# The low part of Q on both partition halves: a second score matmul with 128 rows

## The chip, the cores and the metric

The kernel runs on one core of a Trainium2 chip. The metric is the device time of one execution in microseconds (us). Engines are named as the profile names them: PE is the matmul engine, PEld its weight loads, DVE, ACT and POOL the three elementwise engines, SP the engine whose queue issues every DMA of this kernel.

## The reference, cut to what matters

One encoder layer is computed for a prompt of 512 tokens and a sample of 2048 tokens, both of width 1024. One projection of the normalised input yields everything; branch A is neighbourhood attention on a grid of 64 columns, 8 heads of 64 channels, a window of 8 x 16 keys, a learned bias; branch B is a 2-D DFT, branch C a depthwise convolution. The three are gated, merged and projected.

```python
q, k, v, gate_a, u_b, gate_b, c_val, c_glu, gate_c, merge_a, merge_b, merge_c = split(h @ w_in)
s = einsum('bqhd,bikhd->bhqik', q_row * 64 ** -0.5, k_blk) + bias        # per head, masked to the window
p = softmax(s)
y_a = einsum('bhqik,bikhd->bqhd', p, v_blk) * silu(gate_a)
```

## The kernel before, in words

All matmul operands are held as two float32r parts, high and low, whose sum is the float32 value. A product of two such numbers is high by high, high by low and low by high; the low by low term is left out in most places.

The work is done in chunks of 512 tokens: chunk 0 is the prompt, chunks 1 to 4 the sample. A first pass projects chunks 1 and 2 together, then 3 and 4, then 0; a second pass merges and projects out. Q, K and V leave each projection for DRAM (`qd`, `kd`, `vd`) and come back for attention. `proj_qk` (L282) stores K with one DMA per high and low part (L310), Q with one DMA (L307).

`attention(c)` (L485) is a generator with 112 steps per chunk. It runs over four pairs of heads j; a pair loads its K (`ksp`, L528) and its Q (`qsp`, L530 to L534), both in a single buffer, so that the load for pair j+1 waits for the last score matmul of pair j. Then come four column blocks cb, each with a V load (`vsp`, L545, two buffers) and two heads h. A head's scores come from two matmuls, L553 and L554, over 2, 3 or 4 times 128 keys, so 256, 384 or 512 columns. K of a head holds its high part on partitions 0 to 63 and its low part on 64 to 127. The high part of Q stands on both halves, so L553 gives high Q by high K plus high Q by low K with 128 rows. L554 adds low Q by high K with 64 rows. DVE adds the bias and takes the maximum (L557), ACT exponentiates and scales (L561, L563), PE transposes (L584), and PE multiplies with V (L594) some heads later.

There are 5 chunks with 4 pairs each, so 20 loads of Q, and 20 x 8 = 160 score pairs of L553 and L554.

`task` and `pump` (L255 to L268) mix the steps of generators into the projections: after every six projection matmuls, `pump` emits as many attention steps as are due. The framework's scheduler then orders each engine's queue with a timing model of its own, so the order in the trace isn't quite the source's order. All DMAs stand in one SP queue in that order.

The 20 pairs are numbered 0 to 19 below: 0 to 3 belong to chunk 1, 4 to 7, 8 to 11 and 12 to 15 to chunks 2, 3 and 4, and 16 to 19 to the prompt. The first and second score pair of a head pair are those of cb = 0 with h = 0 and h = 1.

Of the kernel before, what the change touches and what calls it, by code (L numbers as in the profile page):

```python
# [15 lines left out]
F32 = mybir.dt.float32  # L16
# [11 lines left out]
C = 512            # tokens of a chunk: 8 grid rows  # L28
NCH = 5            # chunk 0 is the prompt, 1..4 the sample
# [3 lines left out]
# row patterns of attention: (key quads, first key row relative to the row group - 4, key row of the grid)  # L33
# [7 lines left out]
def attention_masks():  # L41
    """Additive masks [row pattern, query, column pattern, key] of the window."""
    out = np.full((4, P, 3, 512), -1e30, np.float32)
    for mp, (rows, r0, kr0, nq) in enumerate(((8, 0, 0, 2), (32, 0, 0, 3), (32, 8, 4, 4), (32, 24, 20, 3))):
        for cp, cb in enumerate((0, 1, 3)):
            for q in range(P):
                r, c = r0 + q // 16, 16 * cb + q % 16
                rs = min(max(r - 4, 0), rows - 8)
                cs = min(max(c - 8, 0), 48)
                kr = kr0 + np.arange(nq * 4)[:, None]  # L50
                kc = KSTART[cb] + np.arange(32)[None, :]
                ok = (kr >= rs) & (kr < rs + 8) & (kc >= cs) & (kc < cs + 16)
                out[mp, q, cp, : nq * 128] = np.where(ok, 0.0, -1e30).reshape(-1)
    return out.astype(ml_dtypes.bfloat16)


def dft_pairs(n1):
    """The residues k1 of a unit of the position DFT; the others are mirrored ones."""
    h = n1 // 2
    return [(0, h)] + [tuple(range(k, min(k + 2, h))) for k in range(1, h, 2)]  # L60


def dft_tables():
    """Units [128, (k1 of the pair, real and imaginary input, real and imaginary output, 128)], L = 2048 and 512."""
    units = []
    p = np.arange(P, dtype=np.float64)[:, None]
    k2 = np.arange(P, dtype=np.float64)[None, :]
    for n1 in (16, 4):
        L = n1 * P
        for pair in dft_pairs(n1):  # L70
            u = np.zeros((P, 2, 2, 2, P))
            for i, k1 in enumerate(pair):
                a = 2 * np.pi * np.mod(p * (k1 + n1 * k2), L) / L
                c, s = np.cos(a) / math.sqrt(L), np.sin(a) / math.sqrt(L)
                u[:, i, 0, 0], u[:, i, 0, 1] = c, -s
                if k1 % (n1 // 2):
                    u[:, i, 1, 0], u[:, i, 1, 1] = -s, -c
            units.append(u.reshape(P, 1024))
    return np.stack(units).astype(np.float32)
# [12 lines left out]
class Build:  # L92
# [5 lines left out]
    def newton(self, pool, tag, v, eng, steps=3, bufs=2):  # L98
        """v -> 1/sqrt(v) on a tile, through the exponent trick and Newton steps."""
        nc = self.nc  # L100
        shape = list(v.shape)
        y = pool.tile(shape, F32, tag=tag, name="nw_y", bufs=bufs)
        t = pool.tile(shape, F32, tag=tag, name="nw_t", bufs=bufs)
        nc.vector.tensor_scalar(y.bitcast(I32), v.bitcast(I32), 1, None, op0=ALU.logical_shift_right)
        nc.vector.tensor_scalar(y.bitcast(I32), y.bitcast(I32), -1, 0x5F3759DF, op0=ALU.mult, op1=ALU.add)
        if shape[1:] == [1]:
            w = pool.tile(shape, F32, tag=tag, name="nw_w", bufs=bufs)
            nc.vector.tensor_scalar_mul(w, v, -0.5)
            for _ in range(steps):
                nc.vector.tensor_scalar(t, y, y, w, op0=ALU.mult, op1=ALU.mult)  # L110
                nc.vector.scalar_tensor_tensor(y, t, 1.5, y, op0=ALU.add, op1=ALU.mult)  # L111
            return y
        for _ in range(steps):
            eng.tensor_tensor(t, y, y, op=ALU.mult)
            nc.vector.scalar_tensor_tensor(t, t, -0.5, v, op0=ALU.mult, op1=ALU.mult)
            nc.vector.scalar_tensor_tensor(y, t, 1.5, y, op0=ALU.add, op1=ALU.mult)
        return y

    def split(self, dst, src):
        """dst[:, 0] + dst[:, 1] = src."""  # L120
        nc = self.nc
        nc.scalar.copy(dst[:, 0], src)  # L122
        return nc.vector.tensor_tensor(dst[:, 1], src, dst[:, 0].bitcast(F32), op=ALU.subtract)  # L123

    def emit_unit(self, src, pieces=1):
        """A [128, 1024] weight unit, split into its two parts."""
# [8 lines left out]
    def unit(self):  # L135
        """The next unit of the stream; the two behind it are on their way."""
# [4 lines left out]
    def stream(self):  # L141
        """The units of the first pass in their order."""
# [10 lines left out]
    def narrow(self, ps, w, rhs, kts=range(KT)):  # L153
        """ps[128 cols, C] = sum over kts of w[kt]^T rhs[kt], three passes."""
# [11 lines left out]
    def wide(self, ps, ws, lhs, tt):  # L166
        """ps[128 tokens, 256] = sum over kt of lhs[kt][:, tokens]^T w[kt]."""
# [13 lines left out]
    def rstd_rows(self, c, pool, xpool, tag, bufs):  # L181
        """rstd of every token of chunk c, into DRAM as a row; returned by token too."""
# [12 lines left out]
    def make_h(self, c, pool, tiles, ring):  # L195
        """Appends the ring tiles of chunk c: h^T, split."""
# [12 lines left out]
    def raw_h(self, c, tiles, ring):  # L209
        """As make_h, but without rstd: the users of these tiles scale their results."""  # L210
# [18 lines left out]
    def raw_scale(self, c, pool, rrow):  # L229
        """rstd of chunk c, by token (self.rt) and as a row on all partitions (self.rr)."""  # L230
# [24 lines left out]
    def task(self, gen, n, start, end):  # L255
        """Emits gen's n steps evenly between the half units start and end."""
# [17 lines left out]
    def scaled(self, c, ps):  # L274
        """A projection of chunk c from tiles without rstd gets it here."""
# [6 lines left out]
    def proj_qk(self, hs):  # L282
        nc = self.nc
        for j in range(4):
            for dst in (self.kd, self.qd):
                w = self.unit()
                for c, hT in hs.items():
# [12 lines left out]
                    if dst is self.qd:  # L300
                        # the queries of a column block together
# [51 lines left out]
    def proj_c(self, hs, first=()):  # L353
        """first: PSUM tags of the first blocks, where others than mm."""
# [22 lines left out]
    def halo(self, left, right):  # L377
        """Fills the borders of two neighbouring chunks; None stands for the end of the sequence."""
# [43 lines left out]
    def conv(self, c, cb, tail=False):  # L422
        """With tail, the columns that need the right neighbour come in a step of their own, the 21st."""
# [61 lines left out]
    def attention(self, c):  # L485
# [4 lines left out]
        # rows of K by chunk: (chunk, first row in it, rows, first row in the tile)  # L490
# [31 lines left out]
        for j in range(4):  # L522
            kn = 4 * nq * 64
            # K of a head: its high part on one half of the partitions, its low part on the other
# [4 lines left out]
            # Q: the high part of either head on both halves, the low parts of both on the first  # L529
# [4 lines left out]
            nc.sync.dma_start(qsp[:64, 2:].bitcast(F32), lo)  # L534
# [4 lines left out]
            for cb in range(4):  # L539
# [8 lines left out]
                for h in range(2):  # L548
# [5 lines left out]
                    nc.tensor.matmul(s[:, :n], lhsT=qsp[:64, 2 + h, cb], rhs=kk[:64], start=False, stop=True)  # L554
# [35 lines left out]
    def attend(self, c, j, cb, h, nq, vsp, psp, pv, o):  # L590
        """pv[V's high part, V's low part; head; P's high part, P's low part], the latter two added into o."""
# [14 lines left out]
    def fft(self, pool, n1):  # L606
        """The 2-D DFT of the prompt (n1 = 4) or of the sample (n1 = 16)."""
# [12 lines left out]
        for blk in range(2):  # L620
# [4 lines left out]
            # G[k1] as pairs (real part, minus the imaginary part)  # L625
# [12 lines left out]
            else:  # L638
# [9 lines left out]
                # d = b1-b7, b2-b6, b3-b5 ; e = the sums ; f = b'1-b'3, b'1+b'3  # L648
# [68 lines left out]
            def stage_o(i, hs):  # L717
                """The real parts' and the imaginary parts' share: their sum, and their difference mirrored."""
# [32 lines left out]
    def prepare(self, c, hh, pool):  # L751
        """The gated branches of 256 tokens, split."""
# [21 lines left out]
    def merge(self, c, hh, ysp, pool, thp):  # L774
        """The merged branches of 256 tokens, transposed and split (4 times their value)."""
# [25 lines left out]
    def finish(self, c, hh, msp, pool, last):  # L801
        nc = self.nc
        for tt in range(2):
# [16 lines left out]
            # the merged sum carries a factor of 4, the guard 16 with it  # L820
# [14 lines left out]
    def dft_parts(self):  # L835
        """The units of the position DFT, split, into DRAM."""
# [5 lines left out]
    def bias_tables(self):  # L842
        """Bias of (head, query (r, c), key row, key column): Toeplitz in rows and columns."""
# [9 lines left out]
    def run(self):  # L853
        tc, nc, a = self.tc, self.nc, self.a
        with ExitStack() as ctx:
# [31 lines left out]
            # the table of functions is loaded while the first data are on their way  # L887
# [13 lines left out]
            # slots of a half: c 32, q and k 64, v 32, u 16, gates 64, merge gates 192 by two halves  # L901
# [12 lines left out]
            # the first two chunks start before their rstd is known  # L914
# [19 lines left out]
            # first super-chunk  # L934
# [23 lines left out]
            # second  # L958
# [23 lines left out]
            # third: the prompt  # L982
# [62 lines left out]
    def constants(self, cst):  # L1045
# [7 lines left out]
        # the gated input of the convolution carries a factor of 2  # L1053
# [57 lines left out]
```

## Time and profile before

| | |
|---|---|
| Time, median of 3 runs | 2563.64 us (2562.47 to 2572.91) |
| Span of the profiled execution | 2565.2 us |
| Mean granted PE clock | 0.926 of full speed |
| PE busy | 2228.6 us (87%), 11184 matmuls |
| PEld busy | 1836.6 us (72%) |
| DVE busy | 1298.2 us (51%) |
| ACT busy | 779.7 us (30%) |
| POOL busy | 295.9 us (12%) |
| DMA | 399.19 MB, mean 156 GB/s; 47.8% of 16 engines' span |

The profiled execution has no time of its own beside its span; the span lies 1.6 us above the median of the three runs. Matmuls are pipelined, so two neighbours in the trace overlap and the distance between their starts is what one costs. A DMA's time on the SP queue is the time that its issue took, not its transfer. In a table by windows, the DMA share is that of all 16 DMA engines, so 0.13 is two of them.

### The profile page before, as it was taken

Reading aid. Unit: us, or ns where it says so; the run is one execution under the profiler, and the core shown is the slowest. Engines: PE = TensorE matmul, PEld = TensorE weight load, DVE = VectorE, ACT = ScalarE, POOL = GpSimd, SP = SyncE. Lnnn points to the kernel's source line nnn. Section 1 sums busy time; section 2 is a strip of 40 time slices with the busy share of each in tenths; the row PEclk is TensorE's granted clock in tenths of the full one; section 3 lists DMA queues with packets and bytes.
Section 4 is the critical chain, followed back from the end, with each engine's and each line's share of the span. In section 5 each row is a group of like instructions: output and inputs, shape, how many; then the busy total and the mean of one; then the engine's idle time right before and its main releaser. Section 6 shows DMA issues by size and latency. Waiting matters only on the chain. (4 is left out here: it accounts for less than half of the span.)

```text
span 2565.2 us, 30454 instructions
## 1 busy us (share of the span) xinstructions
PE 2228.6 (87%) x11184; PEld 1836.6 (72%) x11184; DVE 1298.2 (51%) x2704; ACT 779.7 (30%) x1479; POOL 295.9 (12%) x286
## 2 busy tenths in 40 slices
PE   8869999999989987887878877766887899999998
PEld 7649877777767875665656655555766788898997
DVE  6235565554344464544443422454764357666665
ACT  5113233333322233433333333322344332111111
POOL 0000010100000011111111101100111012122221
PEclk9889999999999998888888888887998999999999
DMA  7346443443623444343333443436655576555542
GB/s 272 103 148 188 159 160 120 159 150 115 188 75 116 156 148 129 118 142 129 128 119 121 146 148 120 151 119 195 215 176 194 188 265 213 180 177 182 174 156 80
DMA packets 238068, 399.19 MB, mean 156 GB/s; under 512 B 33888, under 2 KB 136928, under 8 KB 235232
## 3 DMA queue, kind: packets, MB, share of 16 engines
q1 hardware_dynamic: 237920, 397.26, 47.8%
q8 instruction: 88, 1.44, 0.2%
q14 instruction: 60, 0.49, 0.1%
HBM read 287.61 MB, written 112.73 MB: 156 GB/s over the span
## 5 line engine op out<-in xcount | busy, mean ns | idle before, releaser
L160 PE MATMUL mm<-hT,w 128*128 128x512 f32 x1760 | 741.1, 421 | 51.2 <-DVE z L295 25.6
L161 PE MATMUL mm<-hT,w 128*128 128x512 f32 x1760 | 722.3, 410 | 0.1
L162 PE MATMUL mm<-hT,w 128*128 128x512 f32 x1760 | 720.1, 409 | 0.8 <-DVE w L123 0.8
L160 PEld LDWEIGHTS mm<-hT,w 128*128 128x128 f32 x1760 | 348.3, 198 | 145.0 <-DVE z L295 26.6
L162 PEld LDWEIGHTS mm<-hT,w 128*128 128x128 f32 x1760 | 348.7, 198 | 83.3 <-issue 2.5
L161 PEld LDWEIGHTS mm<-hT,w 128*128 128x128 f32 x1760 | 349.1, 198 | 69.1 <-issue 1.8
L511 POOL TENSOR_TENSOR bias<-tab,mask 128x384 f32<-128x384 f32 (+2 forms) x160 | 182.7, 1143 | 1623.6 <-DVE m L557 1360.9
L123 DVE TENSOR_TENSOR w<-wraw,w 128x1024 fp32r<-128x1024 f32 (+1 forms) x162 | 203.2, 1255 | 129.8 <-ACT w L122 129.3
L434 DVE SCALAR_TENSOR_TENSOR acc<-cb,cw,acc 128x512 f32<-128x512 f32 (+1 forms) x300 | 242.6, 811 | 2.4
L557 DVE CUSTOM_DVE_ANT_0 p<-s,bias 128x384 f32<-128x384 f32 (+2 forms) x160 | 92.8, 581 | 273.7 <-PE s L554 168.6
L122 ACT CAST w<-wraw 128x1024 fp32r<-128x1024 f32 (+1 forms) x162 | 168.1, 1039 | 141.3 <-PE mm L162 87.6
L160 PE MATMUL mm<-ysp,wb 128*128 128x256 f32 x640 | 181.9, 284 | 4.0 <-DVE th L790 4.0
L161 PE MATMUL mm<-ysp,wb 128*128 128x256 f32 x640 | 181.7, 284 | 0.0
L162 PE MATMUL mm<-ysp,wb 128*128 128x256 f32 x640 | 181.6, 284 | 0.0
L561 ACT ACTIVATE p<-p,m 128x384 f32<-128x384 f32 (+2 forms) x160 | 102.0, 638 | 200.4 <-DVE m L560 197.9
L594 PE MATMUL pv<-psp,vsp 128*128 128x256 f32 x512 | 102.2, 315 | 58.7 <-issue 37.5
L174 PE MATMUL mm<-w,hT 128*128 128x256 f32 x480 | 136.9, 287 | 16.2 <-ACT w L122 14.5
L553 PE MATMUL s<-ksp,qsp 128*128 128x384 f32 (+2 forms) x160 | 63.2, 395 | 93.3 <-DMA qsp<-qd 75.1
L594 PEld LDWEIGHTS pv<-psp,vsp 128*128 128x128 f32 x512 | 86.1, 209 | 75.9 <-issue 52.1
L175 PE MATMUL mm<-w,hT 128*128 128x256 f32 x480 | 137.4, 287 | 0.7 <-DVE w L123 0.7
L176 PE MATMUL mm<-w,hT 128*128 128x256 f32 x480 | 136.8, 285 | 0.0
L160 PEld LDWEIGHTS mm<-ysp,wb 128*128 128x128 f32 x640 | 123.3, 193 | 5.6 <-DVE th L790 4.2
(151 smaller groups left out, 3029.1 us busy)
## 6 DMA issues: line engine op xcount, KB each, us to landing
wraw<-wn SPq DMA_DIRECT2D x135, 512.0 KB
vsp<-vd SPq DMA_DIRECT2D x256, 128.0 KB
th<-z SPq DMA_DIRECT2D x120, 256.0 KB
th<-th SPq DMA_DIRECT2D x80, 384.0 KB
tab<-tabd SPq DMA_DIRECT2D x40, 384.0 KB
qsp<-qd SPq DMA_DIRECT2D x60, 256.0 KB
w<-dftd SPq DMA_DIRECT2D x14, 1024.0 KB
kd<-zs SPq DMA_DIRECT2D x40, 256.0 KB
```

The lines of the kernel that those rows point to most:

```text
L122: nc.scalar.copy(dst[:, 0], src)
L123: return nc.vector.tensor_tensor(dst[:, 1], src, dst[:, 0].bitcast(F32), op=ALU.subtract)
L160: nc.tensor.matmul(ps, lhsT=w[:, 0, s], rhs=r[:, 0], start=n == 0, stop=False)
L161: nc.tensor.matmul(ps, lhsT=w[:, 0, s], rhs=r[:, 1], start=False, stop=False)
L162: nc.tensor.matmul(ps, lhsT=w[:, 1, s], rhs=r[:, 0], start=False, stop=n == len(kts) - 1)
L174: nc.tensor.matmul(ps, lhsT=r[:, 0, q], rhs=w[:, 0, s], start=kt == 0, stop=False)
L175: nc.tensor.matmul(ps, lhsT=r[:, 0, q], rhs=w[:, 1, s], start=False, stop=False)
L176: nc.tensor.matmul(ps, lhsT=r[:, 1, q], rhs=w[:, 0, s], start=False, stop=kt == KT - 1)
L434: nc.vector.scalar_tensor_tensor(acc[:, :n], cb[:, b, e:e + n], wv[:, e:e + 1], acc[:, :n], op0=ALU.mult, op1=ALU.add)
L511: nc.gpsimd.tensor_tensor(bias, tabs[h][:, trow: trow + 4 * nq, RCOL[cb]: RCOL[cb] + 32], mask[:, COLPAT[cb], :n].rearrange("p (r c) -> p ...
L561: nc.scalar.activation(p[:, :n], p[:, :n], AF.Exp, bias=m[:, 1:2], accum_out=m[:, 2:3])
L594: nc.tensor.matmul(pv[:, h], lhsT=vsp[:, i, h], rhs=psp[:, i], start=i == 0, stop=i == nq - 1)
```

## The change

The third load of Q, which put the low parts of both heads on partitions 0 to 63, becomes two loads, one per head, each of which puts a head's low part on both halves. They have the form of the two loads of the high part and alternate with them. L554 takes all 128 rows; it now also adds low Q by low K. The diff also drops comments, which are left out here.

```diff
             for h in range(2):
                 nc.sync.dma_start(qsp[:, h].bitcast(F32), hi[:, h].unsqueeze(0).broadcast_to([2, 64, C]))
-            nc.sync.dma_start(qsp[:64, 2:].bitcast(F32), lo)
+                nc.sync.dma_start(qsp[:, 2 + h].bitcast(F32), lo[:, h].unsqueeze(0).broadcast_to([2, 64, C]))
...
                     nc.tensor.matmul(s[:, :n], lhsT=qsp[:, h, cb], rhs=kk, start=True, stop=False)
-                    nc.tensor.matmul(s[:, :n], lhsT=qsp[:64, 2 + h, cb], rhs=kk[:64], start=False, stop=True)
+                    nc.tensor.matmul(s[:, :n], lhsT=qsp[:, 2 + h, cb], rhs=kk, start=False, stop=True)
```

## Rows read from the trace of the kernel before

**Rows 1.** The page's first lines: span, instructions, busy time of each engine.
```profile
span 2565.2 us, 30454 instructions
PE 2228.6 (87%) x11184; PEld 1836.6 (72%) x11184; DVE 1298.2 (51%) x2704; ACT 779.7 (30%) x1479; POOL 295.9 (12%) x286
```

**Rows 2.** Waits of PE: line <- releaser: us in total, times, longest us.
```profile
PE s L553 <- DMA qsp<-qd: 75.1, 12, 10.9
PE s L554 <- DMA qsp<-qd: 53.7, 14, 6.8
```

**Rows 3.** Timeline of PE near 412 and 1048 us: start, duration, instruction.
```profile
411.95 0.39 PE L162 MATMUL mm<-hT,w 128*128 128x512 f32 x1
412.18 0.34 PE L553 MATMUL s<-ksp,qsp 128*128 128x384 f32 x1
412.45 0.44 PE L554 MATMUL s<-ksp,qsp 64*128 64x384 f32 x1
412.82 0.50 PE L160 MATMUL mm<-hT,w 128*128 128x512 f32 x1
413.16 0.39 PE L161 MATMUL mm<-hT,w 128*128 128x512 f32 x1
...
1048.16 0.40 PE L553 MATMUL s<-ksp,qsp 128*128 128x512 f32 x1
1048.49 0.50 PE L554 MATMUL s<-ksp,qsp 64*128 64x512 f32 x1
1048.92 0.51 PE L162 MATMUL mm<-hT,w 128*128 128x512 f32 x1
1049.27 0.40 PE L160 MATMUL mm<-hT,w 128*128 128x512 f32 x1
1049.50 0.39 PE L161 MATMUL mm<-hT,w 128*128 128x512 f32 x1
```

**Rows 4.** Timeline of PEld, the same stretch at 1048 us.
```profile
1048.49 0.18 PEld L554 LDWEIGHTS s<-ksp,qsp 64*128 64x128 f32 x1 [0.37 <-issue]
1048.92 0.19 PEld L162 LDWEIGHTS mm<-hT,w 128*128 128x128 f32 x1 [0.25 <-issue]
```

**Rows 5.** Timeline of the SP queue, start of pair 10.
```profile
1277.69 4.07 SPq L533 DMA_DIRECT2D qsp<-qd  x2
1281.81 5.04 SPq L534 DMA_DIRECT2D qsp<-qd  x1
...
1288.15 9.09 SPq L545 DMA_DIRECT2D vsp<-vd  x4
```

**Rows 6.** Windows: stretch, length, busy of five engines, PEclk, DMA share, GB/s.
```profile
1017.00:1019.00 2.00, 0.00 (x0) 0.00 (x0) 0.00 (x0) 0.00 (x0) 0.00 (x0) 1.00 0.13 51
1021.00:1023.00 2.00, 0.00 (x0) 0.00 (x0) 0.00 (x0) 0.00 (x0) 0.00 (x0) 0.50 0.98 302
1284.00:1287.00 3.00, 0.00 (x0) 0.00 (x0) 0.19 (x1) 0.00 (x0) 0.00 (x0) 0.72 0.13 50
```

**Rows 7.** Timeline of PE, the first two score pairs of pair 10.
```profile
1291.02 0.77 PE L553 MATMUL s<-ksp,qsp 128*128 128x512 f32 x1 [8.95 <-DMA vsp<-vd]
...
1297.37 0.79 PE L554 MATMUL s<-ksp,qsp 64*128 64x512 f32 x1 [3.45 <-DMA qsp<-qd]
1298.10 0.79 PE L553 MATMUL s<-ksp,qsp 128*128 128x512 f32 x1
1298.82 0.79 PE L554 MATMUL s<-ksp,qsp 64*128 64x512 f32 x1
```

**Rows 8.** Timeline of PE, L554 at the starts of pairs 1, 5 and 19.
```profile
389.96 0.44 PE L554 MATMUL s<-ksp,qsp 64*128 64x384 f32 x1 [3.85 <-DMA qsp<-qd]
401.30 0.44 PE L554 MATMUL s<-ksp,qsp 64*128 64x384 f32 x1
...
964.11 0.92 PE L554 MATMUL s<-ksp,qsp 64*128 64x512 f32 x2 [0.26 <-DMA qsp<-qd]
...
1974.56 0.58 PE L554 MATMUL s<-ksp,qsp 64*128 64x256 f32 x1 [6.85 <-DMA qsp<-qd]
...
1976.86 0.58 PE L554 MATMUL s<-ksp,qsp 64*128 64x256 f32 x1
```

**Rows 9.** Timeline of PE, other waits near loads of Q (pairs 0, 8, 16).
```profile
118.68 0.80 PE L160 MATMUL mm<-hT,w 128*128 128x512 f32 x1 [9.04 <-DVE z L295]
...
1162.92 0.55 PE L594 MATMUL pv<-psp,vsp 128*128 128x256 f32 x1 [9.65 <-DMA vsp<-vd]
...
1749.66 2.93 PE L709 MATMUL hp<-w,fgs 128*128 128x256 f32 x12 [31.54 <-DMA w<-dftd]
```

## The prediction

> **What bounds the kernel now.** I read the busy times first: PE works 87% of the span and no other engine more than 51% of it (its weight loads, 72%, run beside the matmuls) [rows 1]. A saving on PE is therefore worth its full size wherever PE isn't waiting. Next I read PE's waits, because the remaining 13% decide what a DMA is worth: the score matmuls wait for the loads of Q, 75.1 us at L553 and 53.7 us at L554, together 129 us of the some 337 us in which PE is idle [rows 2]. So the change touches both sides of the bound: it shortens PE's work, and it enlarges the very transfer for which PE waits most. Then I read PE's timeline around a score pair (what the 64 rows cost), and SP's timeline with the windows around a load of Q (what one load costs).
>
> **PE: what goes.** In the rows at 1048 us, projection matmuls of 512 columns stand 0.23 us apart (1049.27 to 1049.50). From L553 to L554 it is 0.33 us for the same 512 columns, from L554 to the next matmul 0.43 us, and from there to the one after 0.35 us: 0.10 + 0.20 + 0.12 = 0.42 us over three steps of 0.23 [rows 3]. With 384 columns a step should take three quarters of 0.23, 0.17 us; the distances are 0.27, 0.37 and 0.34 (the last against 0.23): 0.10 + 0.20 + 0.11 = 0.41 us [rows 3]. The excess does not grow with the columns, so it belongs to the switch between 64 and 128 rows. The weight loads say the same: that of L554 and that of the matmul behind it start together with their matmuls, after 0.37 and 0.25 us of idleness, instead of one matmul ahead [rows 4]. With 128 rows on both sides I take all of it to go: 0.40 us x 160 pairs = 64 us. The first two score pairs of a head pair whose Q is late save nothing, because PE waits there anyway; with 11 such head pairs (below) 22 pairs drop out: 0.40 x 138 = 55 us.
>
> The Trainium skill, "TensorE: Matmul & The Clock Gate", section "LDWEIGHTS (loading the stationary operand)", says that a 32x128 weight load takes as long as a 128x128 one, since its columns decide. The durations agree (0.18 and 0.19 us, rows 4), and by that alone nothing would be saved; the distances between starts speak against it. It is a rival below.
>
> **DMA: what comes.** Each of 20 head pairs loads 2 x 256 KB of high parts with L533 and 256 KB of low parts with L534. After the change it is four loads in the form of L533. While the loads of L533 are alone in flight, the DMA share is 0.13, two engines of 16, at 50 to 51 GB/s, where other loads reach 302 GB/s at a share of 0.98 [rows 6]. One such load takes 262,144 B / 50.5 GB/s = 5.2 us. SP shows it too: the two L533 and the L534 behind them hold the queue for 9.1 us [rows 5], because the two engines' queues are full. L534's own form is not the slow one: 256 KB at 302 GB/s are 0.9 us. So the last byte of a head pair's Q lands later by 2 x 5.2 - 0.9 = 9.5 us. Bounds: no less than 5.2 us (if one of the new loads were to spread over 16 engines), no more than 10.4 (if L534 took nothing). I take 9.5, since all four loads have one form and one queue.
>
> The Trainium skill, "DMA: Bandwidth & Descriptors", section "Why a DMA increments its semaphore by 16 and not by 1", says that the number of engines is the largest up to 16 that divides the slowest dimension of both access patterns. The broadcast source begins with a dimension of 2, L534's with 64; the measured share of 0.13 agrees, and by that rule the new loads of the low part take two engines.
>
> **What of it reaches PE.** The order of landing becomes high 0, low 0, high 1, low 1. The first score pair is about as early as now: its low part, now second, lands where high 1 lands today, just before today's L534. The second score pair needs low 1, so it can't start before today's first L554 (released by L534's landing) + 9.5 us. In pair 10 that is 1297.37 + 9.5 = 1306.9, and its L554 ran at 1298.82: 8.0 us more [rows 7]. The same sum for all head pairs whose first L554 now waits for Q: pair 5 has both L554 back to back at 964.1 (+9.2), pair 19 has 1974.56 and 1976.86 (+7.2) [rows 8]. From first to last there are 11 that lose (5, 7, 9, 10, 11, 13, 14, 15, 17, 18, 19), in the order of time 9.2, 8.9, 5.1, 8.0, 4.9, 6.4, 7.4, 8.1, 4.2, 2.7, 7.2: 72 us. Pairs like 1, with 389.96 and 401.30, lose nothing: 11.3 us of projections lie between [rows 8]; so do 2, 3 and 6.
>
> The other starts have no score matmul waiting, but other transfers queue behind Q. In pair 8 the loads of V are issued behind it, and L594 waits 9.65 us for them; pair 12 is alike. In pair 16 a DFT table is queued between the loads of Q and PE waits 31.54 us for it. In pair 0, PE waits 9.04 us for tiles whose stores of K go through DMAs behind Q [rows 9]. Each can grow by up to 9.5 us, and pair 4 by some 5: 43 us at most, none at least. I take 35, as three of these waits end directly on a transfer that is in the queue behind.
>
> What else is queued behind the longer SP issue: weights, stores of gates, V. SP is held some 10 us longer, but low 1 lands later than that issue ends, so PE waits for Q anyway and these aren't late again. The weights are two units ahead.
>
> **Sum.** -55 + 72 + 35 = +52 us on a span of 2565.2. The span lies 1.6 us above the median of the runs, so on that median: 2564 + 52, rounded 2615 us, 2% slower. The scheduler orders the queues by its own model, which neither rows nor diff show; I allow 15 us either way.
>
> **The rivals.**
> 1. *The loads hide, the matmul gain stays (faster).* If the scheduler puts 9.5 us of projections between the first and the second score pair, as pairs 1, 2, 3 and 6 have already, the 72 us go; with only half of the 35 left: 2564 - 64 + 18 = 2518. It decides at a distance of 9.5 us between the two L554. For it: the work exists, PE always has projections at hand. Against: in 11 head pairs the distance is now 0.3 to 6.8 us, and a planner that knew of the slow loads would not have L554 wait 53.7 us [rows 2].
> 2. *The two sides cancel.* Waits behind the loads fall to nearly nothing and half of the 72 is given back, as later stalls of PE shrink: 2564 - 55 + 36 + 20 = 2565. For it: PE has other short idle times that could absorb.
> 3. *Everything is exposed.* All 20 starts lose both loads in full, since the two engines carry their sixteenth of all other transfers too: 20 x 10.4 - 50 = +158, so 2722. For it: the share of 0.13 shows a queue with no slack while Q is on its way. Against: pairs 1, 2, 3 and 6.
> 4. *The matmul gain fails.* The 0.40 us belong to the score matmuls' accumulation or to their strided keys, not to the rows: 2564 + 72 + 35 = 2671. Against: the matmul after L554 pays as well, with no such operands [rows 3]. The skill's rule on weight loads above would mean this case.
>
> **How the numbers follow.** The forecast (own range 2580 to 2650) gets 0.52, rival 1 0.16, rival 2 0.12, rival 3 0.12, rival 4 0.08. Faster by over 0.5% (about what a measurement of this kernel can tell from no change) is rival 1: 0.16. Within it is rival 2: 0.12. Slower are the rest: 0.72. For eight in ten I go from 2535, which leaves out most of rival 1, to 2690, which takes in rival 4 and leaves out rival 3.
>
> **What would show it.** Right: PE's distances L553 to L554 and onward near 0.23 us for 512 columns, and the weight loads one matmul ahead; two engines busy (0.13) for some 20 us at each start of a head pair instead of 10; new waits of PE for Q at the second score pair, with a total of waits for Q near 129 + 72 = 200 us; four loads of Q holding SP for 15 us and more. Wrong: waits for Q that don't grow, or distances that stay at 0.33 and 0.43 us, or a DMA share well above 0.13 while the new loads are in flight.

## The result and the profile after

The changed kernel takes 2661.4 us (median of 4 runs, 2655.1 to 2663.3) against 2563.9 us before: a ratio of 1.0363, 95% interval 1.0341 to 1.0385, so 97 us or 3.6% slower. 2615 us were forecast, with a range of 2535 to 2690. The direction and the mechanism held; the loss is nearly twice the 52 us of the sum, and the experiments below say which terms were mis-sized. The time lies above the forecast's own range of 2580 to 2650 us and only 10 us from the 2671 us of rival 4, in which the matmul gain fails. So the time alone does not speak for the forecast; the traces have to decide.

The page of the changed kernel, its span and busy times, answers to [rows 1]:

```profile
span 2653.3 us, 30477 instructions
...
PE 2181.4 (82%) x11184; PEld 1846.1 (70%) x11184; DVE 1294.1 (49%) x2704; ACT 778.3 (29%) x1479; POOL 295.1 (11%) x286
```

PE is busy for 47 us less with the same number of matmuls, and the span is 88 us longer: PE's idle time rose from 337 to 472 us. The busy time shrank where it was expected to. The timeline of PE at a score pair of 512 columns, then that of its weight loads, answer to [rows 3, 4]:

```profile
1346.40 0.39 PE L162 MATMUL mm<-hT,w 128*128 128x512 f32 x1
1346.63 0.40 PE L553 MATMUL s<-ksp,qsp 128*128 128x512 f32 x1
1346.87 0.40 PE L554 MATMUL s<-ksp,qsp 128*128 128x512 f32 x1
1347.10 0.39 PE L160 MATMUL mm<-hT,w 128*128 128x512 f32 x1
1347.34 0.39 PE L161 MATMUL mm<-hT,w 128*128 128x512 f32 x1
```

```profile
1346.41 0.19 PEld L553 LDWEIGHTS s<-ksp,qsp 128*128 128x128 f32 x1
1346.63 0.19 PEld L554 LDWEIGHTS s<-ksp,qsp 128*128 128x128 f32 x1
1346.87 0.19 PEld L160 LDWEIGHTS mm<-hT,w 128*128 128x128 f32 x1
```

From L553 on, the starts are 0.24, 0.23 and 0.24 us apart, where they were 0.33, 0.43 and 0.35. The weight load of L554 now starts with L553's matmul, one matmul ahead of its own. The durations of the weight loads are as before (0.19 us); only their starts moved. The price of the switch of rows, 0.4 us a pair, is gone.

The SP queue and PE at the start of pair 10, and two windows of that start, answer to [rows 5 to 7]:

```profile
1307.76 0.64 SPq L533 DMA_DIRECT2D qsp<-qd  x1
1308.52 2.91 SPq L534 DMA_DIRECT2D qsp<-qd  x1
1311.47 4.99 SPq L533 DMA_DIRECT2D qsp<-qd  x1
1316.51 5.08 SPq L534 DMA_DIRECT2D qsp<-qd  x1
```

```profile
1320.25 0.76 PE L553 MATMUL s<-ksp,qsp 128*128 128x512 f32 x1 [8.10 <-DMA qsp<-qd]
...
1325.36 0.80 PE L554 MATMUL s<-ksp,qsp 128*128 128x512 f32 x1 [3.49 <-DMA qsp<-qd]
...
1331.12 0.76 PE L553 MATMUL s<-ksp,qsp 128*128 128x512 f32 x1 [3.69 <-DMA qsp<-qd]
...
1336.06 0.80 PE L554 MATMUL s<-ksp,qsp 128*128 128x512 f32 x1 [3.32 <-DMA qsp<-qd]
```

```profile
1316.00:1319.00 3.00, 0.00 (x0) 0.00 (x0) 0.00 (x0) 0.00 (x0) 0.00 (x0) 0.50 0.13 51
...
1323.00:1325.00 2.00, 0.00 (x0) 0.00 (x0) 0.00 (x0) 0.00 (x0) 0.00 (x0) 0.50 0.13 50
...
1310.00:1336.00 26.00, 7.46 (x24) 4.44 (x22) 6.71 (x11) 0.86 (x2) 1.59 (x1) 0.60 0.27 92
```

This is the forecast in one picture: SP is held 2.9 to 5.1 us by each of the three loads behind the first (13.6 us by all four, where 15 and more were forecast), the DMA share is 0.13 at 50 to 51 GB/s, and the four score matmuls start 5.1, 5.8 and 4.9 us apart, each as its own load lands. From the first to the last of them it is 15.8 us, where it was 7.8. Taken the same way, from the first L553 to the second L554, the starts of the 11 head pairs that were to lose 72 us grew by some 79 us, in ten of them by what was forecast to within 1 us. In pair 7 it was 14 us instead of 8.9; there four loads of V, 12.4 us of issue, stand between the third and the fourth load of Q.

The longest window adds something that was not in the sum: over 26 us PE's granted clock is 0.60. In the kernel before, 26 us from about the same point of pair 10 had 0.67:

```profile
1279.00:1305.00 26.00, 13.60 (x47) 9.43 (x46) 8.74 (x16) 2.88 (x7) 2.74 (x2) 0.67 0.38 123
```

PE's waits, in total, answer to [rows 2, 9]; behind them stand the waits before product, table and projection matmuls in the timeline of PE:

```profile
PE s L554 <- DMA qsp<-qd: 109.4, 27, 8.2
PE s L553 <- DMA qsp<-qd: 100.9, 22, 9.1
PE hp L709 <- DMA w<-dftd: 55.5, 5, 30.7
...
PE mm L160 <- DVE z L295: 36.4, 5, 19.2
PE pv L594 <- DMA vsp<-vd: 34.8, 10, 17.6
```

```profile
126.15 0.79 PE L160 MATMUL mm<-hT,w 128*128 128x512 f32 x1 [19.15 <-DVE z L295]
...
695.75 1.01 PE L594 MATMUL pv<-psp,vsp 128*128 128x256 f32 x3 [13.81 <-DVE psp L587]
...
1191.75 0.55 PE L594 MATMUL pv<-psp,vsp 128*128 128x256 f32 x1 [17.63 <-DMA vsp<-vd]
...
1482.72 0.55 PE L594 MATMUL pv<-psp,vsp 128*128 128x256 f32 x1 [10.33 <-DMA vsp<-vd]
...
1819.37 1.86 PE L709 MATMUL hp<-w,fgs 128*128 128x256 f32 x7 [30.75 <-DMA w<-dftd]
...
1846.63 2.69 PE L709 MATMUL hp<-w,fgs 128*128 128x256 f32 x11 [13.17 <-DMA w<-dftd]
```

The waits for Q grew from 129 to 210 us. Some waits at the first score matmul of a head pair stand under other names (8.9, 6.9 and 2.4 us before, 4.0 us after); with them it is 147 and 214. Of the five starts that the prediction put under other waits, pair 0's wait grew from 9.0 to 19.2 us and pair 8's from 9.7 to 17.6; pair 4's, 3.5 us at L594 before, to 13.8; pair 12 has a wait for V of 10.3 us where the longest was 0.9. In pair 16 the first table came no later, but the next one did: 13.2 us instead of 4.1. One reading was wrong: in pair 12 the score matmuls did wait for Q, 3.5 and 5.3 us before and 2.6 and 4.7 us after. It changes nothing in the sum, as the second score pair stood 13 us behind the first.

### The profile page after: what moved, and what is told of

It reads as the page before. It is cut to its first block, busy times and chain, and to the rows that moved or that the text cites. A ratio compares the mean times of both kernels' runs of the same rounds, so it can differ in the third digit from the quotient of the medians.

```text
span 2653.3 us, 30477 instructions
## 1 busy us (share of the span) xinstructions
PE 2181.4 (82%) x11184; PEld 1846.1 (70%) x11184; DVE 1294.1 (49%) x2704; ACT 778.3 (29%) x1479; POOL 295.1 (11%) x286
## 5 line engine op out<-in xcount | busy, mean ns | idle before, releaser
L557 DVE CUSTOM_DVE_ANT_0 p<-s,bias 128x384 f32<-128x384 f32 (+2 forms) x160 | 92.5, 580 | 317.6 <-PE s L554 190.9
L594 PE MATMUL pv<-psp,vsp 128*128 128x256 f32 x512 | 102.2, 316 | 99.7 <-issue 48.8
L594 PEld LDWEIGHTS pv<-psp,vsp 128*128 128x128 f32 x512 | 86.5, 211 | 116.8 <-issue 81.9
L553 PE MATMUL s<-ksp,qsp 128*128 128x384 f32 (+2 forms) x160 | 64.1, 401 | 112.7 <-DMA qsp<-qd 100.9
L554 PE MATMUL s<-ksp,qsp 128*128 128x384 f32 (+2 forms) x160 | 66.1, 413 | 109.4 <-DMA qsp<-qd 109.4
L174 PE MATMUL mm<-w,hT 128*128 128x256 f32 x480 | 135.7, 285 | 13.6 <-ACT w L122 12.8
```

The source lines that it names most:

```text
L174: nc.tensor.matmul(ps, lhsT=r[:, 0, q], rhs=w[:, 0, s], start=kt == 0, stop=False)
L594: nc.tensor.matmul(pv[:, h], lhsT=vsp[:, i, h], rhs=psp[:, i], start=i == 0, stop=i == nq - 1)
```

## Experiments

Ratios are to the kernel before on the same chip, whose median was 2569.2 us beside E1 to E4, 2568.9 beside E5 to E8 and 2569.5 beside E9 to E12. The theories: A, the added loads cost what they cost because a broadcast load runs on two of 16 engines; B, it is one more load and 256 KB more a head pair, however written; C, TensorE gains nothing from the rows. "By halves" means two transfers of 64 partitions each: one half of the partitions with both heads or both parts at a time, so that neither side begins with a dimension of 2.

**E1: 128 rows, the low part loaded by halves.** Number of loads and bytes as in the changed kernel.

```diff
-                nc.sync.dma_start(qsp[:, 2 + h].bitcast(F32), lo[:, h].unsqueeze(0).broadcast_to([2, 64, C]))
+                nc.sync.dma_start(qsp[64 * h: 64 * h + 64, 2:].bitcast(F32), lo)
```

> The matmul half of the change alone: L554 has 128 rows as in the changed kernel, but the low parts of both heads reach the two partition halves by two loads of 64 partitions each, without a broadcast; number of loads (4 a head pair) and bytes are those of the changed kernel. Theory A (the added loads cost what they cost because a broadcast load runs on two of 16 DMA engines): the added load takes about 0.9 us instead of 5.2, so the waits for Q stay at some 130 us as in the kernel before and the matmul gain of 47 to 64 us stands: 2500 to 2520 us. Theory B (one more load and 256 KB more a head pair cost it, however they are written): as the changed kernel, 2640 to 2680 us. Theory C (no gain on TensorE, rival 4): about 2564 us.

Measured: 2559.6 us, ratio 0.9968 (0.9955 to 0.9980). B falls: the same bytes in as many loads cost 101 us less than by broadcast. But A missed its 2500 to 2520 us too: PE is busy for 53 us less (2175.7 us) and only 8 us come out. The waits for Q had grown:

```profile
PE s L553 <- DMA qsp<-qd: 122.2, 19, 10.7
...
PE s L554 <- DMA qsp<-qd: 45.2, 12, 7.0
```

**E2: the broadcast loads, 64 rows.**

```diff
-                    nc.tensor.matmul(s[:, :n], lhsT=qsp[:, 2 + h, cb], rhs=kk, start=False, stop=True)
+                    nc.tensor.matmul(s[:, :n], lhsT=qsp[:64, 2 + h, cb], rhs=kk[:64], start=False, stop=True)
```

> The load half of the change alone: the four broadcast loads of the changed kernel, but L554 takes the 64 rows of the kernel before (the copy of low Q on the upper half is loaded and not read). Theory A: the matmul gain is missing from the changed kernel's time, 2661 + 47 to 64 = 2708 to 2725 us, and the distances of 0.33, 0.43 and 0.35 us around L554 are back. Theory C (no gain on TensorE): 2661 us. If gain and loss don't add (the gain falls into waits), something between.

Measured: 2689.7 us, ratio 1.0469 (1.0451 to 1.0488): the loads alone cost 120 us. The timeline of PE in this run has the old distances back, and its page has PE busy for 20 us longer than before:

```profile
1366.89 0.40 PE L553 MATMUL s<-ksp,qsp 128*128 128x512 f32 x1
1367.22 0.50 PE L554 MATMUL s<-ksp,qsp 64*128 64x512 f32 x1
1367.65 0.50 PE L160 MATMUL mm<-hT,w 128*128 128x512 f32 x1
1367.99 0.40 PE L161 MATMUL mm<-hT,w 128*128 128x512 f32 x1
```

```profile
PE 2249.0 (84%) x11184; PEld 1846.6 (69%) x11184; DVE 1294.0 (48%) x2704; ACT 778.9 (29%) x1479; POOL 294.4 (11%) x286
```

The changed kernel is 28 us below this, not 47 to 64. C falls, but so does a full gain.

**E3: 128 rows, all four loads by halves. E4: 64 rows, the high part by halves, the old low load.** E3 has E1's edit and this one; E4 has this one with the old L534 and L554.

```diff
-                nc.sync.dma_start(qsp[:, h].bitcast(F32), hi[:, h].unsqueeze(0).broadcast_to([2, 64, C]))
+                nc.sync.dma_start(qsp[64 * h: 64 * h + 64, :2].bitcast(F32), hi)
```

> L554 with 128 rows, and all four loads of Q of 64 partitions each, without a broadcast: high parts too. Theory A: the loads of the high part fall from 2 x 5.2 to 2 x 0.9 us, the last of Q lands about 8.6 us earlier than in the run with the low part alone by half, and most of the 129 us of waits for Q goes: 2385 to 2430 us. Theory B: as the changed kernel, 2640 to 2680 us. If waits behind the score matmuls take over (V, the copies of P), 2430 to 2490 us.

> The kernel before with its two broadcast loads of the high part replaced by two loads of 64 partitions each; L554 keeps its 64 rows and the one load of the low part stays. Theory A: the waits for Q of 129 us go for the most part, 2435 to 2480 us, and the difference to the run with all loads by half and 128 rows is the matmul gain alone, now without waits to hide in: 60 to 66 us. Theory B: as the kernel before, 2564 us.

Measured: E3 2423.7 us, ratio 0.9443 (0.9424 to 0.9462); E4 2428.1 us, 0.9456 (0.9441 to 0.9470). Taking the two broadcasts of the high part away is worth 141 us at 64 rows, a little more than the 129 us of waits for Q [rows 2]. While Q's loads by halves are in flight in E4, with other transfers, the DMA share is 1.09 and not 0.13:

```profile
1215.00:1217.00 2.00, 1.67 (x11) 1.15 (x9) 1.49 (x3) 0.86 (x2) 0.00 (x0) 1.00 1.09 243
```

A holds, though E4 lies 7 us below its range. The matmul gain of 60 to 66 us that was expected between E3 and E4 did not appear: the times differ by 4 us. Three things differ there: the rows of L554, a second copy of the low part, and the order of the loads, in which E3 has a low part between the two high ones (E6 and E7 take them apart).

**E5: 128 rows without a second copy of the low part.** The old load, into a tile whose upper half is zeroed once a chunk (so low Q by low K is again left out). This parts the rows from the loads. Theory D: the second copy as such ate the gain in E1. Theory E: PE's saving turns into a longer wait for Q.

```diff
+        qlo = pool.tile([P, 2, C], F32R, tag="qlo", name="qlo", bufs=1)
+        nc.gpsimd.memset(qlo[64:].bitcast(F32), 0.0)
...
+            nc.sync.dma_start(qlo[:64].bitcast(F32), lo)
...
+                    nc.tensor.matmul(s[:, :n], lhsT=qlo4[:, h, cb], rhs=kk, start=False, stop=True)
```

> The matmul half alone with the loads of the kernel before, byte for byte: the low part of Q stands on the lower half by the old load, in a tile whose upper half is zeroed once a chunk, and L554 takes all 128 rows. No load is added. In the run with the low part by half the waits of PE grew by nearly what its work shrank, and only 8 us of 53 came out. Theory D (there the second copy of the low part cost the rest, even spread over 16 engines: some 2 us later a head pair): 2500 to 2520 us here. Theory E (a shorter score matmul can't shorten a head pair, since the next load of Q is released by a chain through DMA, V and the softmax, and PE's saving turns into a longer wait for Q): 2545 to 2565 us, with waits of L553 and L554 for Q longer by 30 to 50 us than the 129 us of the kernel before.

Measured: 2533.8 us, ratio 0.9864 (0.9845 to 0.9884): 35 us, between the theories. The page has PE busy for 2164.2 us, 64 less than before, as the 0.40 us x 160 said. Below it stand the waits of the two score matmuls (L556 and L557 in this file) and of the product with V, then two waits of the kernel before:

```profile
PE 2164.2 (86%) x11184; PEld 1838.8 (73%) x11184; DVE 1295.4 (51%) x2704; ACT 779.6 (31%) x1479; POOL 303.1 (12%) x291
...
PE s L556 <- DMA qsp<-qd: 70.3, 10, 10.4
PE s L557 <- DMA qlo<-qd: 55.6, 15, 6.3
PE pv L597 <- issue: 47.1, 11, 7.1
...
PE s L556 <- DMA ksp<-kd: 23.9, 5, 7.4
```

```profile
PE pv L594 <- issue: 37.5, 10, 6.5
...
PE s L553 <- issue: 6.9, 1, 6.9
```

With 9.6 us that are put down to a weight load, the score matmuls wait 159 us in E5. Counted in the same way, under all names, they waited 147 us before (129, 8.9 and 6.9 us, and 2.4 under DVE). So they wait 12 us longer, not the 30 to 50 of theory E, and the product with V 11 us longer, under all names. Both theories have a part: about half of PE's saving comes out, and E1 is 27 us slower than E5 (by the ratios). Those 27 us are not the second copy alone, since in E1 a low part also stands between the two high ones.

**E6: E5 with the high part by halves. E7: E3 with both high loads ahead of both low loads.**

> As the run with zeros, but the high parts loaded by two loads of 64 partitions each, without a broadcast; against the run with the high part by half and 64 rows (2428 us) only the rows of L554 differ. Theory D: the matmul gain comes out where Q is early, 2370 to 2385 us. Theory E: 2410 to 2428 us.

> The four loads of 64 partitions of the run with all by half (2424 us), but both loads of the high part first, then both of the low part; L554 with 128 rows. If the first L553 there waits for three loads of which it needs two, it starts some 1.3 us earlier here in each of 13 head pairs while the last load lands when it did: 2405 to 2420 us. If the last landing decides: 2424 us, no change.

Measured: E6 2390.4 us, ratio 0.9305 (0.9285 to 0.9325), 38 us below E4, between the ranges of D and E again and nearer to D; so an early Q alone doesn't release the rest. E7 2402.5 us, 0.9351 (0.9320 to 0.9383), 21 us below E3 (expected 4 to 19): the order of the loads counts. All waits of the score matmuls fall from 86 us in E3 to 73, which fits that the first of them waited there for three loads of which it needs two; it is only a part of the 21 us. With the order equal, the second copy of the low part costs some 12 us (E7 against E6).

**E8: E6 with the stores of K and of the attention output by halves.** Their destinations began with a dimension of 2, too. In the kernel before, the share is 0.13 while stores of K are in flight (and 0.13 at 52 GB/s from 994 to 996 us, with stores of the output):

```profile
115.00:122.00 7.00, 3.32 (x8) 2.64 (x9) 2.71 (x4) 0.62 (x1) 0.00 (x0) 0.50 0.13 50
```

```diff
-                    for i in range(2):
-                        nc.sync.dma_start(dst[c][j, :, i], z[:, i].bitcast(F32))
+                    for h in range(2):
+                        nc.sync.dma_start(dst[c][j, h].rearrange("i p t -> p i t"), z[64 * h: 64 * h + 64].bitcast(F32))
...
-            for h in range(2):
-                nc.sync.dma_start(self.ya[c][j].rearrange("i (h p) t -> i p h t", h=2)[:, :, h], o[:, h])
+            for i in range(2):
+                nc.sync.dma_start(self.ya[c][j][i].rearrange("(h p) t -> p h t", h=2), o[64 * i: 64 * i + 64])
```

> As the run with zeros and the high part by half, and besides the stores of K and of the attention output written by half, 64 partitions each, where the destination began with a dimension of 2 before. If the number of DMA engines follows that dimension for stores too, the waits at L160 for tiles that such stores hold (26 us in the kernel before) and at L594 for the output tile go: 20 to 50 us below the run with zeros and the high part by half. If not, no change against it.

Measured: 2186.9 us, ratio 0.8511 (0.8490 to 0.8533), 203 us below E6; the direction was right and the size wrong by four times. It is the fastest version here. Its page:

```profile
span 2179.2 us, 30452 instructions
...
PE 2084.2 (96%) x11184; PEld 1788.3 (82%) x11184; DVE 1294.2 (59%) x2704; ACT 780.5 (36%) x1479; POOL 302.3 (14%) x291
```

PE's idle time falls to 95 us, and PE's own time by another 56 us with the same matmuls: the mean granted clock is 0.981, against 0.947 in E6, where PE idles for 246 us.

**E9 and E10: E6 with the stores of K alone, and with those of the output alone.**

> The run with zeros and the high part by half (2390 us), with the stores of K alone written by half. The run with both stores by half stood at 2187, 203 us lower, far more than the 20 to 50 expected. If the stores of K make it: 2200 to 2250 us, and the waits at L160 for z (20 us) and for the DFT tables (33 us) go. If those of the attention output make it: 2320 to 2350 us, since only these two waits go.

> The run with zeros and the high part by half (2390 us), with the stores of the attention output alone written by half. They stand in the queue just ahead of the loads of Q. If they make most of the 203 us: 2220 to 2260 us, with the waits at the product with V (48 us) gone. The two single runs should add up to the joint one within 20 us.

Measured: E9 2308.5 us, ratio 0.8983 (0.8966 to 0.9000), 82 us below E6; E10 2275.3 us, 0.8859 (0.8829 to 0.8889), 115 us below. They add up to 197 of the 203. Neither kind of store makes most of the gain: E9 lies between its two ranges and E10 15 us above its own. In E9 the 33 us of waits for DFT tables fall to 9 and those for z vanish; in E10 the wait of the product with V falls from 48 to 2.2 us, and with it ACT's wait for the output tile that the store holds, from 98.5 to 10 us. From the waits of all engines, E6 first, then E9, then E10:

```profile
ACT ob L602 <- DMA ya<-ob: 98.5, 12, 13.7
...
PE pv L597 <- issue: 48.1, 11, 6.7
...
PE hp L712 <- DMA w<-dftd: 32.8, 5, 20.8
...
PE mm L160 <- DVE z L295: 19.7, 6, 8.1
```

```profile
PE hp L712 <- DMA w<-dftd: 8.9, 3, 4.2
```

```profile
ACT ob L602 <- DMA ya<-ob: 10.0, 6, 5.0
...
PE pv L597 <- issue: 2.2, 1, 2.2
```

**E11 and E12: the changed kernel and the kernel before, both with E8's stores.**

> The changed kernel with the stores of K and of the attention output written by half, so that the broadcast loads of Q are almost alone on the two engines. Against the kernel before with the same stores. If the added loads cost by their own length (two loads of 5.2 us in place of one of 0.9): the difference stays at 80 to 110 us. If they cost because they stand in one queue with the two-engine stores: it falls below 60 us.

> The kernel before with the stores of K and of the attention output written by half, the loads of Q as they were: the partner of the changed kernel with these stores. 200 us less than the kernel before, 2340 to 2390 us, if the gain of the stores does not depend on the loads of Q.

Measured: E11 2445.2 us, ratio 0.9516 (0.9500 to 0.9532); E12 2353.2 us, 0.9162 (0.9145 to 0.9180). The change costs 92 us here and 97 without the new stores, inside the 80 to 110 us of the first theory. The added loads cost by their own length, hardly by these stores in their two queues.

## Why the prediction was right, and where its sizes were off

*Removed: the switch of rows.* Right, and well sized as work: 0.40 us x 160 pairs = 64 us were forecast, and PE's busy time falls by 64 us in E5. What failed is the sentence that a saving on PE "is worth its full size wherever PE isn't waiting". 55 us were put into the sum; 35 come out alone (E5), 38 with an early Q (E6 against E4), 28 beside the slow loads (E2 against the changed kernel). PE's waits give the rest back: in E5 PE idles for 30 us more than before, 12 at the score matmuls, 11 at the product with V and the rest in small parts. A likely reason is that a head pair is not PE alone: the next load of Q stands in the SP queue behind V loads and the output's stores, whose release comes through DMA and ACT, so PE waits longer when it gets there sooner. E10 shows that a store on two engines is behind the wait at the product with V. How much of what was given back this chain accounts for was not tried.

*Added: the two-engine loads.* Right in kind (E1, E4) and in length: 5.1, 5.8 and 4.9 us between the four score matmuls for the 5.2 us of the sum, and in pair 10 the last score matmul stands 15.8 us behind the first, where [rows 7] and the step of 9.5 us gave 6.35 + 9.5 = 15.9. The waits for Q grew by 81 us by name, or by 67 with those under other names; 72 were forecast. The loads as a whole were put at 72 + 35 = 107 us and cost 120 (E2). In E2's profile, PE's idle time is 442 us against 337 (2691.2 - 2249.0 busy), so 106 us more. That this meets the 107 of the sum is partly luck: some 58 of them are waits for Q (under all names) instead of 72, and the other 48 stand where 35 were taken (in the changed kernel's trace pairs 0, 4, 8, 12 and 16 lose about 10, 10, 8, 10 and 8 us; for pair 4 no more than 5 had been allowed). What the sum had no term for is the clock: PE's own time rises by 20 us in E2 with the same matmuls, at a mean granted clock of 0.901 against 0.926. More of them run at 1.2 GHz around the longer waits, as the windows with 0.60 and 0.67 show for pair 10.

*The sum.* -55 + 107 = +52 became -28 + 120 = +92 in the experiments and 97 as measured. Of the 40 us missing, the matmul term was 27 too large, and the load term lacked 13. The 20 us of the clock are large enough for these; no run takes the clock apart from the waits.

*The rivals.* The loads did not hide (rival 1): the second score pairs stand where they stood, right behind the first. Nothing cancelled (rival 2): the waits behind the loads grew by some 46 us instead of falling. Rival 3 fails as pairs 1, 2, 3 and 6 lose nothing from the first L553 to the second L554. Rival 4, whose 2671 us come nearest to the measured time, falls with the distances and with E5, in which the rows alone take 64 us off PE's busy time and 35 us off the time. Rule and trace agree on the number of engines: by the Trainium skill ("DMA: Bandwidth & Descriptors", "Why a DMA increments its semaphore by 16 and not by 1") a slowest dimension of 2 on either side leaves at most two engines; the share of 0.13 says two. E1, E4 and E8 move the same bytes in as many transfers without that dimension, and bear it out for loads and stores.

## What to carry to other kernels

Before a load is duplicated by a broadcast, look at the DMA share while it runs alone: 0.13 means that two engines carry it, and a load of 256 KB took 5.2 us, where the 302 GB/s of other loads would give 0.9 (an estimate). Writing the same bytes as two transfers of 64 partitions was worth 141 us for the high part of Q and 203 us for two kinds of stores here, far more than any change of the matmuls. And a saving on the busiest engine need not come out in full: here 28 to 38 of 64 us did. Look for what ends the wait at the start of the next round before booking it.

## What the runs showed that I had not expected

Stores of 256 KB, for which PE hardly waited by name, were worth 203 us. PE idles for 151 us less in E8 than in E6: 50 at the product with V, which the store reaches in two steps, through the tile that it holds and then through ACT; some 45 at the projections, 33 at the DFT tables and 25 at the score matmuls. The slow clock became rarer along with these waits: the same 11184 matmuls take 2084.2 us of PE's time in E8, where they take 2140.7 in E6.
